# Decoder layer on one core: other portions in TensorE's written order, and the output weights split once and kept in DRAM

## The chip, the cores and the metric

The kernel runs on one core of one Trainium2 chip. The metric is the device time of one execution in microseconds (us). Before the change the median of three runs is 2806.22 us (2804.65 to 2808.27).

## What is computed

One layer of a hybrid decoder on 2048 tokens of width 1024, in float32:

```python
h = rmsnorm(x)
hg_p, rw_p = split(h @ w_in)              # 1024 x 3840, 30 column tiles of 128
o_hg = hgrn2(hg_p)                        # 4 heads, chunkwise gated linear recurrence
o_rw = rwkv7(token_shift_mix(rw_p))       # 8 heads, chunkwise, inverse of a triangular 64x64 matrix
x = x + concat(o_hg, o_rw) @ w_out        # 1024 x 1024
x = x + conv_ffn(rmsnorm(x))              # up to 2 x 2816, conv of width 3, SiLU gate, down
return rmsnorm(x)
```

Every large product is made of three products: an operand is split into `hi` (a cast to float32r on ScalarE) and `lo` (the rest, a subtraction on VectorE), and `mm3` adds hi x hi, hi x lo and lo x hi. One such triple of 128x512 matmuls is called a dense step below.

## The kernel before

The first part of the kernel (`phase1`, some 1,420 of 2,806 us) interleaves three Python generators: `dense()` (the input projection, block by block of 512 tokens, and for the first three blocks the output projection `out_block`), `rw_stream()` (eight "supers", two in each token block, of the RWKV recurrence) and `hg_stream()` (sixteen units of the HGRN recurrence). The second part (output projection of the last block, feed-forward, final norm) isn't touched by the change.

**Order.** TensorE's instructions stand in the order in which the generators emit them; a scheduling layer places those of the other engines, whose queues then run in order too. The loop at the end of `phase1` takes one step of the RWKV stream and one of the HGRN stream, and then lets `fill` emit dense work for `FLOOR + RATE * (work of these steps)` ns, 900 + 0.45 times. The work is a count kept by the wrapper `Metered`: `V.ns` grows by 150 ns + 1.04 ns an element for each VectorE instruction and by half of that for each ScalarE `act`; and at the two places where `rw_super` sends data through DRAM `V.ns += TRIP_NS` adds 8,000.

**The inverse's round trips.** In `rw_super`, VectorE masks the scores into `M` (from TensorE's line 737). Pieces of `M` go to DRAM and come back as `E` (lines 753, 756: first trip). Thirty-one pairs of VectorE instructions (`etmp`, `Ti`) invert the triangles; `Ti` goes to DRAM and comes back as `TZ` and `TTs` (lines 815 to 828: second trip), and then TensorE goes on at line 836. Between the two trips stand the transposes `KBT` (line 763), those of `AT` (772) and the product `lv` (789), which don't need `E`.

**The output projection.** `out_block` runs over two halves of the block's tokens (`i2`), two halves of the columns (`dh`) and eight k tiles. For each k it loads a tile of w_out (128x512 float32, 256 KB, line 409, by GpSimd's DMA queue), splits it on ScalarE (line 269) and VectorE (line 80), and makes two dense steps with it. So each block loads and splits 32 tiles, the three blocks 96. The pool gives four buffers each to the raw tile, `wh` and `wl`. The rows of `oT` (the recurrences' output) are split as they come in.

**The input projection.** In the first token block `load` reads two raw tiles of 256 KB for each column tile, splits them and stores hi and lo as `Win` in DRAM (four stores of 256 KB); the later blocks load the split tiles. All of these go by GpSimd's queue. SyncE's queue carries the rest, in program order.

## Time and profile before

| | |
|---|---|
| median of 3 runs | 2806.22 us |
| the profiled execution | 2807.51 us |
| its span, first to last instruction | 2805.7 us |
| mean granted TensorE clock | 0.971 |
| TensorE / VectorE / ScalarE busy | 94% / 68% / 49% |
| DMA, mean over the span | 184 GB/s |

All places in time are microseconds from the span's start. "PE" is TensorE, "DVE" VectorE, "ACT" ScalarE, "POOL" GpSimd, "SP" SyncE; DMA queue q0 is GpSimd's and q1 SyncE's. A window row has the window, its length, the busy time of PE, weight loads, DVE, ACT and POOL with instructions in brackets, the granted clock as a share of full speed, the share of the 16 DMA engines in use, and GB/s. A matmul at half clock counts as busy for its longer time, so the time that a window loses on TensorE is its idle time plus length x (1 - clock).

### The profile page before, as it was taken

The page shows a single profiled execution, that of the slowest core. Times are in us where ns is not written, and L with a number is a line of the kernel's source. Part 1 is how long each engine was busy: PE and PEld are TensorE (multiplying, and loading weights), DVE is VectorE, ACT ScalarE, POOL GpSimd, SP SyncE. Part 2 cuts the span into 40 slices and gives each one's busy share as a digit, 9 for nine tenths or more (in the row PEclk, how much of TensorE's full clock was granted, in tenths as well). Part 3 has the DMA queues.
Part 4 walks back from the last instruction along what each step waited for, and adds up shares of the span by engine and source line. Part 5 has one row for each costly group of instructions (what it writes and reads, how often), then busy time and mean ns, then how long its engine had stood idle before and what let it go on. Part 6 is the DMA issues. An engine that isn't in the chain of part 4 may idle for free.

```text
span 2805.7 us, 47910 instructions
## 1 busy us (share of the span) xinstructions
PE 2643.6 (94%) x18059; PEld 2109.4 (75%) x18059; DVE 1910.3 (68%) x3665; ACT 1366.7 (49%) x2178; POOL 367.1 (13%) x660
## 2 busy tenths in 40 slices
PE   7989999998999989989789999998999999999998
PEld 5867777776777767767567888886888888877887
DVE  4856656476545664746667789988998777667656
ACT  4545543454544444434446765446555555445444
POOL 6432222112221122222100000000000000000000
PEclk9989999998999999989899999999999999999999
DMA  8654635346473455844556357755663223999865
GB/s 292 210 154 141 193 117 152 96 134 192 155 197 114 119 158 192 302 117 128 141 186 216 122 161 257 250 187 190 216 226 116 75 89 109 326 323 329 290 193 187
DMA packets 387709, 515.78 MB, mean 184 GB/s; under 512 B 121759, under 2 KB 218389, under 8 KB 387477
## 3 DMA queue, kind: packets, MB, share of 16 engines
q1 hardware_dynamic: 335537, 343.29, 38.5%
q0 software_dynamic: 51872, 169.41, 18.7%
q8 instruction: 142, 2.33, 0.3%
q14 instruction: 90, 0.74, 0.1%
q10 hardware_dynamic: 68, 0.02, 0.0%
HBM read 375.22 MB, written 137.36 MB: 183 GB/s over the span
## 4 chain that ended last, share of the span: by engine, by line
PE 41%; DMA 3%; DVE 3%; issue 1%; ACT 1%; SPq 1%; DVEq 0%; ACTq 0%
PE ua L285 5%; PE ua L287 5%; PE ua L286 5%; PE ud L285 3%; PE ud L286 3%; PE ud L287 3%; PE da L286 2%; PE da L287 2%; PE da L285 2%; PE db L285 2%; PE db L286 2%; PE db L287 2%; PE ub L285 1%; PE ub L287 1%; PE ub L286 1%
## 5 line engine op out<-in xcount | busy, mean ns | idle before, releaser
L285 PE MATMUL pj<-hh,wh 128*128 128x512 f32 x960 | 411.0, 428 | 0.1
L287 PE MATMUL pj<-hh,wl 128*128 128x512 f32 x960 | 380.2, 396 | 0.0
L286 PE MATMUL pj<-hl,wh 128*128 128x512 f32 x960 | 380.1, 396 | 0.0
L285 PE MATMUL ua<-Bh,uwh 128*128 128x512 f32 x704 | 278.5, 396 | 16.2 <-ACT uwh L269 14.1
L287 PE MATMUL ua<-Bh,uwl 128*128 128x512 f32 x704 | 276.5, 393 | 0.5 <-DVE uwl L80 0.4
L286 PE MATMUL ua<-Bl,uwh 128*128 128x512 f32 x704 | 276.1, 392 | 0.0
L285 PEld LDWEIGHTS pj<-hh,wh 128*128 128x128 f32 x960 | 183.6, 191 | 51.5 <-issue 8.8
L286 PEld LDWEIGHTS pj<-hl,wh 128*128 128x128 f32 x960 | 183.9, 192 | 41.0 <-issue 7.7
L287 PEld LDWEIGHTS pj<-hh,wl 128*128 128x128 f32 x960 | 183.2, 191 | 40.9
L269 ACT CAST uwh<-uraw 128x512 fp32r<-128x512 f32 x220 | 134.6, 618 | 145.4 <-PE ua L286 71.7
L269 ACT CAST dah<-draw 128x512 fp32r<-128x512 f32 x151 | 93.9, 622 | 184.5 <-PE da L286 50.5
L80 DVE TENSOR_TENSOR uwl<-uraw,uwh 128x512 fp32r<-128x512 f32 x220 | 146.7, 684 | 50.2 <-ACT uwh L269 50.1
L80 DVE TENSOR_TENSOR dal<-draw,dah 128x512 fp32r<-128x512 f32 x151 | 104.0, 689 | 103.9 <-ACT dah L269 103.5
L285 PEld LDWEIGHTS ua<-Bh,uwh 128*128 128x128 f32 x704 | 133.2, 189 | 45.7 <-ACT uwh L269 14.7
L287 PEld LDWEIGHTS ua<-Bh,uwl 128*128 128x128 f32 x704 | 133.2, 189 | 30.8 <-DVE uwl L80 2.8
L286 PEld LDWEIGHTS ua<-Bl,uwh 128*128 128x128 f32 x704 | 133.4, 190 | 26.9
L285 PE MATMUL ud<-Bh,uwh 128*128 128x512 f32 x352 | 137.9, 392 | 1.4 <-DVE cv L80 1.4
L287 PE MATMUL ud<-Bh,uwl 128*128 128x512 f32 x352 | 137.1, 389 | 0.0
L286 PE MATMUL ud<-Bl,uwh 128*128 128x512 f32 x352 | 137.0, 389 | 0.0
L80 DVE SCALAR_TENSOR_TENSOR y<-cv,cvt,y 128x1024 f32<-128x1024 f32 x88 | 112.5, 1278 | 33.9 <-ACT y L143 33.9
L286 PE MATMUL da<-dbl,dah 128*128 128x512 f32 x340 | 133.4, 392 | 1.1 <-DVE dbl L80 0.9
L287 PE MATMUL da<-dbh,dal 128*128 128x512 f32 x340 | 132.4, 390 | 0.0
(536 smaller groups left out, 6058.4 us busy)
## 6 DMA issues: line engine op xcount, KB each, us to landing
uraw<-in_w_up_dram SPq DMA_DIRECT2D x176, 256.0 KB, 3.2
woraw<-in_w_out_dram POOLq DMA_DIRECT2D x96, 256.0 KB, 3.4
draw<-Sg SPq DMA_DIRECT2D x88, 256.0 KB, 3.3
draw<-Tw SPq DMA_DIRECT2D x88, 256.0 KB, 5.3
gd<-y SPq DMA_DIRECT2D x86, 256.0 KB, 2.9
xt<-x1d SPq DMA_DIRECT2D x32, 512.0 KB, 5.9
draw<-gd SPq DMA_DIRECT2D x63, 256.0 KB, 4.5
draw<-in_w_down_dram SPq DMA_DIRECT2D x63, 256.0 KB, 5.4
```

The costliest lines, as they stand in the source:

```text
L80: return call(out_, *args, **kw)
L269: S.copy(hi, src)
L285: TE.matmul(acc, lh, rh, start=first, stop=False, skip_group_check=skip)
L286: TE.matmul(acc, lh, rl, start=False, stop=False, skip_group_check=skip)
L287: TE.matmul(acc, ll, rh, start=False, stop=last, skip_group_check=skip)
```

## The change

Three edits, all in `phase1`:

1. The portions. VectorE's count and ScalarE's are kept apart, ScalarE's in full, and the larger of the two counts. The trip's constant is 14,000 in place of 8,000, is added only at the second trip, and comes on top of the larger count.
2. `split_wout`, a new generator that is driven by one step for each dense step from the third column tile on: for each half `dh` it loads the 2 MB of w_out into the buffer tag of `M`, splits them into tiles of the tags `KBT`, `KB`, `UV` and `AR` (which the first super uses later) and stores them to `Wod` in DRAM, 1 MB a store, all by SyncE's queue. Each of the sixteen 128x512 pieces is split once.
3. `out_block` loads hi and lo of `Wod` (2 x 256 KB for each k, GpSimd's queue) and splits nothing of w_out. It takes k in pairs: both k for the first 128 tokens, then both for the second.

```diff
-OP_NS, ELEM_NS, TRIP_NS = 150.0, 1.04, 8000.0
+OP_NS, ELEM_NS, TRIP_NS = 150.0, 1.04, 14000.0
...
+    def take(self):
+        t_ = max(self.ns, self.act_ns) + self.wait_ns
+        self.ns = self.act_ns = self.wait_ns = 0.0
+        return t_
...
-        V.ns += 0.5 * (OP_NS + ELEM_NS * width(out_))
+        V.act_ns += OP_NS + ELEM_NS * width(out_)
...
-                        raw = wp.tile([P, 512], F32, tag="wraw", name="woraw", bufs=4)
-                        wload(raw, w_out[0, k * P:(k + 1) * P, dh * 512:dh * 512 + 512])
-                        wh, wl = split(wp, raw, [P, 512], "w", 4)
...
+                    for k2 in range(0, KD, 2):
+                        ws = []
+                        for k in (k2, k2 + 1):
...
+                            w = tuple(wp.tile([P, 512], F32R, tag="w" + c, name="wo" + c, bufs=4) for c in "hl")
+                            for t_, d_ in zip(w, Wod[dh][k // 4]):
+                                wload(t_.bitcast(F32), d_[:, k % 4, :])
+                            ws.append(w)
                         for q in range(2):
...
+                            for k, w in zip((k2, k2 + 1), ws):
...
+                                mm3(accs[q], lhs, w, k == 0, k == KD - 1)
...
+        def split_wout():
+            for dh in range(2):
+                raw = rp.tile([P, 8, BLK], F32, tag="M", name="wod")
+                for q in range(2):
+                    dma(raw[:, 4 * q:4 * q + 4, :],
+                        w_out[0, q * 512:q * 512 + 512, dh * 512:dh * 512 + 512].rearrange("(k p) c -> p k c", p=P))
+                for _ in range(8):
+                    yield
+                for q in range(2):
+                    hi, lo = (rp.tile([P, 4, BLK], F32R, tag=tag, name="wo" + c)
+                              for tag, c in ((("KBT", "h"), ("KB", "l")), (("UV", "h"), ("AR", "l")))[q])
+                    for k in range(4):
+                        split_to(hi[:, k, :], lo[:, k, :], raw[:, 4 * q + k, :])
+                        yield
+                    for t_, d_ in zip((hi, lo), Wod[dh][q]):
+                        dma(d_, t_.bitcast(F32))
...
+                    if i > 1:
+                        next(early, None)
...
-            V.ns += TRIP_NS          # after E<-Ed
...
-            V.ns += TRIP_NS          # after TTs<-T1d
+            V.wait_ns += TRIP_NS
...
-            fill(FLOOR + RATE * (V.ns - t0))
+            fill(FLOOR + RATE * V.take())
```

What this does to the queues is shown at three places.

ScalarE's queue in the first 40 us, before: `hh` are the eight evictions of the transposed first block, of which each dense step of the first column tile needs one, and `wh` the casts of input weights.

```order
L143 ACTIVATE hh<-hg,vt 128x512 x2
L143 ACTIVATE hh<-rw,vt 128x512 x4
L269 CAST wh<-wraw 128x512
L143 ACTIVATE hh<-hg,vt 128x512 x2
L269 CAST wh<-wraw 128x512
```

And after the change, where `woh` are the casts of w_out:

```order
L148 ACTIVATE hh<-hg,vt 128x512 x2
L148 ACTIVATE hh<-rw,vt 128x512
L267 CAST woh<-wod 128x512 x4
L148 ACTIVATE hh<-rw,vt 128x512
L267 CAST woh<-wod 128x512
L148 ACTIVATE hh<-rw,vt 128x512
L267 CAST woh<-wod 128x512 x3
L148 ACTIVATE hh<-rw,vt 128x512
L274 CAST wh<-wraw 128x512
L148 ACTIVATE hh<-hg,vt 128x512 x2
```

Eight casts of w_out now stand among the evictions that the first column tile waits for.

SyncE's queue at the start, before: after the constants come three small weights, the next token block's rows (`xt`) and then the first super's first trip (`Ed`).

```order
L514 DMA cst<-in_consts_dram 128x1344
L512 DMA w2a_195<-in_rw_w_dram 64x512
L513 DMA w2a_195<-in_rw_a_dram 64x512
L515 DMA g_196<-in_rw_g_dram 128x512
L437 DMA xt<-in_x_dram 128x1024 x4
L753 DMA Ed<-M 32x16x32 x4
```

And after it (`wod` are the loads of w_out, 1 MB each; `Wod` the stores, 128x2048 float32, 1 MB each):

```order
L544 DMA cst<-in_consts_dram 128x1344
L448 DMA wod<-in_w_out_dram 128x4x512 x2
L542 DMA w2a_195<-in_rw_w_dram 64x512
L543 DMA w2a_195<-in_rw_a_dram 64x512
L545 DMA g_196<-in_rw_g_dram 128x512
L459 DMA Wod00h<-woh 128x2048
L459 DMA Wod00l<-wol 128x2048
L459 DMA Wod01h<-woh 128x2048
L459 DMA Wod01l<-wol 128x2048
L448 DMA wod<-in_w_out_dram 128x4x512 x2
L467 DMA xt<-in_x_dram 128x1024 x2
L459 DMA Wod10h<-woh 128x2048
```

Three more stores and the other two `xt` follow: four loads and eight stores of 1 MB have come in ahead of the first super.

VectorE's queue where the first super begins, before: `W`, the first super's table of decays, is set at the very start of the program, since its buffer (tag `UV`) is free.

```order
L80 MEMSET eps_73 128x1
L80 MEMSET epsgn 128x1
L80 MEMSET rows 128x128
L80 MEMSET W 128x16
L80 MEMSET Sf 128x256
```

And after it, some 60 rows later, in the fifth and sixth column tile of the first block:

```order
L80 COPY lastc<-pj 128x1
L80 TENSOR_TENSOR wol<-wod,woh 128x512
L80 TENSOR_TENSOR wl<-wraw,wh 128x512 x2
L80 SCALAR_TENSOR_TENSOR rkv_621<-pj,vt,rkv_621 128x511
L80 SCALAR_TENSOR_TENSOR rkv_621<-lastc,vt,rkv_621 128x1
L80 COPY lastc<-pj 128x1
L80 TENSOR_TENSOR wl<-wraw,wh 128x512
L80 MEMSET W 128x16
L80 TENSOR_TENSOR wl<-wraw,wh 128x512
```

The `MEMSET W` has moved behind the last split of w_out (`wol`), and it needs the buffer from which `Wod11h` is stored, so that store has to be over before VectorE goes on to the next `wl`.

On TensorE the portions have moved as follows; the numbers are dense steps, counted in the written order, for supers 0 to 7:

| dense steps | before | after |
|---|---|---|
| between the transposes of KB and those of AT (the portion behind the first trip) | 8, 9, 0, 9, 8, 9, 8, 9 | 3, 3, 4, 4, 3, 3, 3, 3 |
| between `lv` and the product that needs `TZ` (line 836) | 43, 41, 40, 40, 43, 40, 43, 39 | 46, 43, 43, 43, 47, 42, 47, 41 |
| in all between the last scores (line 737) and line 836 | 65, 68, 58, 65, 64, 65, 65, 66 | 64, 64, 65, 64, 65, 62, 65, 62 |

Between the first and the last `etmp` of supers 3, 5 and 7 VectorE's queue held 16, 13 and 13 subtractions of w_out before and holds none after.

60 lines of the change are left out of this document (30 added, 30 removed).

## The prediction

> **What bounds the kernel now.** I read the page's first lines, then windows of the first part, then TensorE's waits in them, and then the DMA queues of the same windows. TensorE is the engine that everything else feeds:
>
> ```profile
> PE 2643.6 (94%) x18059; PEld 2109.4 (75%) x18059; DVE 1910.3 (68%) x3665; ACT 1366.7 (49%) x2178; POOL 367.1 (13%) x660
> ```
>
> So a change pays where it takes away TensorE's idle time, or time at half clock. The second part isn't touched. For the first, one quiet window, and the three windows in which the output projection of blocks 0, 1 and 2 runs:
>
> ```profile
> 1250.00:1320.00 70.00, 69.83 (x520) 52.49 (x517) 43.23 (x83) 29.70 (x40) 18.12 (x34) 1.00 0.40 128
> 581.00:673.00 92.00, 74.53 (x505) 56.12 (x505) 66.60 (x169) 42.05 (x65) 18.95 (x36) 0.91 0.60 169
> 965.00:1057.00 92.00, 75.60 (x876) 57.92 (x875) 64.08 (x163) 39.01 (x69) 17.91 (x34) 0.90 0.57 162
> 1329.00:1417.00 88.00, 73.56 (x872) 56.11 (x871) 56.72 (x149) 41.10 (x72) 14.14 (x27) 0.90 0.51 143
> ```
>
> The quiet window loses nothing. The three others are idle for 17.5, 16.4 and 14.4 us, and by their clock (0.91, 0.90, 0.90) lose another 8.3, 9.2 and 8.8: **74.6 us in all**; at full clock and without idle time they hold 66.2, 66.4 and 64.8 us of work. TensorE's waits over the whole first part name the sources:
>
> ```profile
> PE rw L836 <- DMA TZ<-T0d: 40.7, 12, 10.1
> PE pj L285 <- ACT wh L269: 16.2, 8, 5.3
> PE pj L286 <- DVE wl L80: 7.0, 15, 2.4
> PE rw L886 <- ACT UV L143: 5.7, 2, 3.1
> ```
>
> The first row is the inverse's second trip (12 waits, 40.7 us, the longest 10.1), the next two are the split of weights. The same waits in the first and second block's windows alone:
>
> ```profile
> PE rw L836 <- DMA TZ<-T0d: 0.7, 1, 0.7
> ...
> PE rw L836 <- DMA TZ<-T0d: 3.9, 1, 3.9
> ```
>
> So only some 5 of the trip's 40.7 us lie in the blocks: the blocks and the trips are two stores of lost time. An idle spell also costs clock: the window after super 0's trip runs at 0.61, that of super 6 at 0.60.
>
> ```profile
> 148.00:165.00 17.00, 6.56 (x87) 5.71 (x86) 2.49 (x8) 3.37 (x7) 3.11 (x5) 0.61 0.74 181
> 1200.00:1217.00 17.00, 7.32 (x84) 5.81 (x82) 3.35 (x12) 3.04 (x7) 1.82 (x4) 0.60 0.64 137
> ```
>
> **Part 1: no split of w_out in the blocks.** Removed are 96 casts and 96 subtractions, less 16 of each that are made once:
>
> ```profile
> L409 POOL DMA_DIRECT2D woraw<-in_w_out_dram x96: 537/537/539, 306.9 to 1416.8; - x96
> L269 ACT CAST wh<-woraw x96: 597/619/627, 572.3 to 1420.1; 128x512 fp32r<-128x512 f32 x96
> L80 DVE TENSOR_TENSOR wl<-woraw,wh x96: 628/691/694, 574.0 to 1420.8; 128x512 fp32r<-128x512 f32 x96
> ```
>
> That is 80 x 0.619 = 50 us of ScalarE and 80 x 0.691 = 55 us of VectorE. Neither bounds by itself, but both queues run in order and VectorE is nearly full just where the inverse needs it:
>
> ```profile
> 618.40:660.90 42.50, 38.00 (x115) 0.92 0.52 161
> 792.40:818.40 26.00, 24.50 (x91) 1.00 0.56 191
> ```
>
> The first row is VectorE from the first to the last `etmp` of super 3, beside output block 0: 38.00 of 42.50 us busy. The second is super 4, without a block: 24.50 of 26.00. The sixteen subtractions that leave the first stretch are 16 x 0.69 = 11 us; in supers 5 and 7 thirteen leave, 9 us. So TensorE's waits for weights and the inverse's chain get shorter together, by similar amounts.
>
> What takes the place is DMA. Each k brings 512 KB where 256 KB came. The DMA rows of the three windows (packets, MB, share of the 16 engines):
>
> ```profile
> q0 software_dynamic: 2767, 9.05, 31.9%
> q1 hardware_dynamic: 12257, 6.39, 27.5%
> ...
> q0 software_dynamic: 2640, 8.65, 30.8%
> q1 hardware_dynamic: 12256, 6.16, 25.2%
> ...
> q0 software_dynamic: 2154, 7.06, 26.8%
> q1 hardware_dynamic: 12420, 5.42, 23.6%
> ```
>
> A block's 32 further tiles are 8.39 MB on q0. For the time that this needs there are two rates. By the windows' own (block 0: 0.319 x 92 = 29.3 us for 9.05 MB) q0 would need 56.5, 55.8 and 51.6 us. By the full stretch from 33 to 63 us, where 349 GB/s went at a share of 0.97, so 360 GB/s at 1.00 (row in part 2), it needs 48.4, 47.3 and 42.9. With q1's own 25.3, 23.2 and 20.8 us the DMA engines want 82, 79 and 72 us at the first rate and 74, 71 and 64 at the second, against TensorE's 66, 66 and 65. So **the blocks turn from waiting for the split to waiting for DMA**, and can't shrink to TensorE's own work. I take the middle of the two rates, 78 + 75 + 68 = 221 us, and 9 us more for the trips: with TensorE 13 to 20 us earlier in each block but the chain only 9 to 11 us shorter, some 2 us of wait at line 836 come back, three times, and half as much again in clock. 272 - 230 = **42 us won**. The bounds: 272 - 197 - 9 = 66 us if the transfers hide wholly; 272 - 233 - 9 = 30 at the slower rate. The pairs of k hold a buffer for three of four dense steps, so the loads can't start earlier than that; this is in the same bounds.
>
> **Part 2: the early copy.** The change adds 4 loads and 8 stores of 1 MB, 12.6 million bytes, on SyncE's queue before the first super. What the DMA engines do there:
>
> ```profile
> 21.00:33.00 12.00, 11.03 (x48) 7.72 (x47) 6.33 (x9) 5.46 (x10) 5.32 (x9) 1.00 0.56 178
> 33.00:63.00 30.00, 30.00 (x134) 24.83 (x133) 13.27 (x29) 12.17 (x21) 20.15 (x33) 1.00 0.97 349
> 63.00:69.00 6.00, 6.00 (x27) 3.81 (x26) 3.36 (x6) 3.79 (x7) 2.97 (x6) 1.00 0.81 274
> 69.00:81.00 12.00, 12.00 (x48) 8.54 (x47) 11.33 (x15) 11.89 (x15) 3.46 (x7) 1.00 0.37 127
> ```
>
> From 33 to 63 us TensorE is never idle, and the DMA engines are full with the loads and `Win` stores that keep it fed. Free before 63 us are 0.44 x 12 + 0.03 x 30 = 6.2 us, at 360 GB/s 2.2 MB. `MEMSET W` stands in VectorE's queue ahead of the next input weights and waits for the store of `Wod11h`, so all but that last store's successor (1 MB) must be over there; two of four `xt` loads (1 MB) move behind. 12.6 - 2.1 - 2.2 = 8.3 MB have no room: 23 us at 360 GB/s, which TensorE waits, since its own weights share the engines. The eight casts among the `hh` evictions (8 x 0.62 = 5 us) lie within the same wait. I take **20 us lost**, as the copies can use moments in which the other queue waits. The bounds: 35 us if nothing overlaps (12.6 / 0.360), 8 us if the room from 63 to 81 us (1.1 + 7.6 us) and one buffered column tile (8 dense steps of 0.67 us, 30.00 / 134 x 3) cover the rest.
>
> **Part 3: the portions.** The dense work is the same in sum; it moves between places. What covers both trips together goes from 516 to 511 steps over the eight supers, so the "longer portion" at the second trip is paid for by the one taken away at the first. Outside the blocks' supers (0, 1, 2, 4, 6) the cover changes by -1, -4, +7, +1 and 0 steps, +3 x 0.67 = 2 us, half as much again for clock: **3 us won**, between -10 (every step lost at a wait, none gained) and +12 (the seven steps of super 2 all meet its wait, 4.7 us, and take its clock along, and 4 and 6 gain about as much by a lighter VectorE).
>
> **Sum.** 2807.5 (the profiled execution, span 2805.7) - 42 + 20 - 3 = 2782.5. This execution lies 1.3 us above the median shown, so 2781; I say **2782 us**.
>
> **Two rules that speak against it.** GpSimd issues twice as many loads. The Trainium skill, "SBUF — State Buffer", section "SBUF: two separate sides", says that VectorE in some modes keeps GpSimd from writing the descriptors of its DMAs. By that rule the 64 issues of a block would be stretched beside a full VectorE. The rows say otherwise here: 96 issues took 537 to 539 ns each, in stretches with VectorE 89% busy. I give it no term. The skill's "DMA: Bandwidth & Descriptors", section "Where 436 GB/s comes from", puts the limit of transfers from HBM at about 358 GB/s and that of the fabric at 435; by the first the blocks stay bound by DMA as worked out above, by the second they would hide and the first rival below would hold. The trace's 349 GB/s agrees with the first, as a mean over 30 us.
>
> **The rivals.**
>
> ```profile
> GB/s 229 382 421 426 404 344 290 404 388 415 410 382 426 355 371 415 361 404 333 300 404 300 322 388 350 300 366 344 328 361 333 268 344 344 257 322 350 262 180 382
> ```
>
> *The transfers hide.* For it: in the window from 33 to 63 us several slices of 0.75 us carried over 400 GB/s, as the row shows, and the loads run ahead by two k. Against: at both rates the shares above come to more than TensorE's work nearly everywhere. It gives 2807.5 - 66 + 8 - 3 = 2747. Chance 0.15.
>
> *The inverse takes the place of the weights.* The blocks shrink only by what VectorE is relieved, 11 + 9 + 9 = 29 us, and TensorE waits the rest at line 836. For it: the chain of super 3 is as long as TensorE's path. 2807.5 - 29 + 20 - 3 = 2795.5. Chance 0.15.
>
> *The early copy costs all of its bytes, and the blocks run at the slower rate.* 2807.5 - 30 + 35 - 3 = 2809.5, no change. Chance 0.12.
>
> *The weights land too late: slower.* A pair of k gives its buffers back at three quarters of its four steps, and they are wanted again two pairs later; with a block's 66 us over eight such rounds a load may take 8.3 x 5/8 = 5.2 us, less one issue 4.7. Landing times before:
>
> ```profile
> DMA to landing us min/median/max: 2.8/3.4/6.7
> ...
> Win171l<-wl POOLq DMA_DIRECT2D x1, 256.0 KB, 8.1
> ```
>
> The first row is `woraw`'s, with room; the second a `Win` store of 256 KB in the full stretch. Each us above 4.7 costs 24 rounds x 1.5 (clock) = 36 us. From 6.1 us on (the 66 + 3 - 20 = 49 us that would else be won, by 36, above 4.7) the change loses; at 6.5 us the time is 2807.5 - 66 + 65 + 20 - 3 = 2823, at 7 us 2841. Chance 0.18.
>
> The forecast itself keeps 0.40. Differences under 0.2%, 5.6 us, can't be told from no change. Faster: the forecast (nearly all of it), the first two rivals and a little of the third: 0.68. Same: most of the third and edges of the others: 0.13. Slower: 0.19. The range of 2750 to 2822 us takes in the bounds of the blocks and of the early copy and the near end of the last rival.
>
> **What would show it.** Right: windows of the output blocks of 74 to 80 us with a DMA share above 0.8 and no waits for casts; `etmp` stretches near 30 us in supers 3, 5 and 7; TensorE idle some 20 us before 100 us with a DMA share near 1, and VectorE idle ahead of `W`. Wrong: TensorE not idle early (the copies hid), or block windows as long as now with waits on `woh` and `wol` for DMA (the last rival) or on `TZ` (the second).

## The result, and the profile after

| | before | after |
|---|---|---|
| median of 5 runs | 2806.22 us (2804.65 to 2812.06) | 2822.57 us (2814.95 to 2825.03) |
| ratio, 95% interval | 1 | 1.0048 [1.0030, 1.0067] |
| the profiled execution | 2807.51 us | 2814.95 us |
| its span / mean granted clock | 2805.7 us / 0.971 | 2813.1 us / 0.975 |

The kernel became slower by 0.3 to 0.7%, where 24 us were forecast to be won. The profiled execution of after is the fastest of its five, so its span is only 7.4 us longer than that of before; a second profile of the same kernel (`changed_again` below) has 2821.0 us, and its stretches differ by no more than 5 us from those read here.

The page's first line has the engines' busy time in the whole execution:

```profile
PE 2639.5 (94%) x18059; PEld 2101.1 (75%) x18059; DVE 1861.9 (66%) x3585; ACT 1320.3 (47%) x2096; POOL 418.6 (15%) x756
```

The work that was to go is gone: VectorE has 48.4 us less, ScalarE 46.4. TensorE has the same. So the question is what TensorE waits for now. I cut the first part at the first matmul of each super (`rw<-tl,w2a`), which the change doesn't touch, and compare stretches. Windows of before from the starts of supers 3, 5 and 7 to those of 4, 6 and of the second part, in which the three output blocks lie, and the same of after:

```profile
550.90:741.70 190.80, 173.18 (x1530) 131.74 (x1529) 114.94 (x264) 87.01 (x134) 38.96 (x73) 0.94 0.54 160
897.20:1112.50 215.30, 195.29 (x1649) 151.10 (x1648) 120.92 (x283) 94.32 (x149) 45.04 (x84) 0.94 0.52 158
1277.20:1445.00 167.80, 147.52 (x1447) 111.60 (x1446) 106.17 (x249) 75.14 (x119) 27.86 (x52) 0.95 0.47 141
```

```profile
565.20:754.50 189.30, 167.70 (x1515) 127.23 (x1513) 94.69 (x232) 70.79 (x102) 56.05 (x106) 0.95 0.66 203
903.80:1117.90 214.10, 193.93 (x1658) 148.95 (x1656) 102.35 (x253) 73.83 (x115) 63.20 (x119) 0.96 0.63 198
1278.70:1449.40 170.70, 149.47 (x1458) 112.63 (x1456) 87.78 (x220) 53.60 (x84) 47.62 (x89) 0.96 0.62 189
```

The second column is the length: 573.9 us before, 574.1 after. **The blocks' stretches won nothing.** Length less TensorE's busy time is 57.9 us before and 63.0 after; length times the missing clock is 32.7 and 24.9. The whole span adds up like this (after minus before): +16.9 us up to the start of super 1; -2.6 in supers 1 and 2, -6.2 in super 4 and -3.9 in super 6, which hold no block; +0.2 in the three blocks' stretches; +4.9 between the first two weights of the second part (`wacc` to `ua`); -1.8 after that.

TensorE's waits of the whole first part, after; shown are the second trip, the cast of `hh` and all rows with block weights (total us, times, longest):

```profile
PE rw L868 <- DMA TZ<-T0d: 26.5, 7, 8.1
PE pj L290 <- DMA woh<-Wod11h: 12.5, 7, 6.4
...
PE pj L290 <- ACT hh L267: 7.8, 1, 7.8
...
PE pj L290 <- DMA woh<-Wod10h: 4.9, 5, 2.2
PE pj L291 <- DMA wol<-Wod10l: 4.0, 5, 1.7
...
PE pj L291 <- DMA wol<-Wod11l: 3.2, 7, 1.2
PE pj L291 <- DMA wol<-Wod01l: 3.0, 3, 1.4
...
PE pj L290 <- DMA woh<-Wod01h: 2.4, 4, 1.3
...
PE pj L290 <- DMA woh<-Wod00h: 0.9, 1, 0.9
```

The casts' rows (16.2 and 7.0 us before) are gone, and in their place stand 30.9 us of waits for `woh` and `wol` to land. The waits for the inverse's second trip fell from 40.7 to 26.5 us, but not in the blocks: in their three stretches they were 4.6 us and are 3.6. The landing times of these loads, and of `woraw` before, are in the groups of their lines:

```profile
DMA to landing us min/median/max: 3.1/4.9/7.9
```

Before they were 2.8/3.4/6.7. The DMA engines are not full meanwhile; windows inside the three blocks (the column before the last is the DMA share), and GpSimd's queue in the first of them:

```profile
590.00:690.00 100.00, 82.23 (x651) 62.48 (x650) 53.74 (x151) 27.53 (x42) 36.08 (x69) 0.91 0.84 247
965.00:1070.00 105.00, 88.58 (x972) 66.69 (x971) 53.10 (x155) 26.49 (x47) 36.14 (x68) 0.95 0.75 230
1329.00:1420.00 91.00, 75.26 (x921) 56.75 (x919) 41.77 (x128) 21.74 (x42) 32.42 (x61) 0.96 0.75 228
```

```profile
q0 software_dynamic: 5388, 17.65, 57.5%
```

17.65 MB took 57.5 us of full share, 307 GB/s: the slower of the two rates that the prediction used. But the longest wait has another reason than the rate. GpSimd's queue at the end of block 0, and TensorE's matmul behind it:

```profile
670.59 0.54 POOL L616 DMA_DIRECT2D wl<-Win280l  x1 [5.10 <-PE pj L291]
671.12 0.54 POOL L616 DMA_DIRECT2D wh<-Win280h  x1
672.04 0.54 POOL L616 DMA_DIRECT2D wh<-Win281h  x1 [0.38 <-PE pj L292]
672.57 0.54 POOL L616 DMA_DIRECT2D wl<-Win281l  x1
674.11 0.54 POOL L417 DMA_DIRECT2D woh<-Wod11h  x1 [1.01 <-PE pj L292]
674.64 0.54 POOL L417 DMA_DIRECT2D wol<-Wod11l  x1
```

```profile
680.93 0.79 PE L290 MATMUL pj<-woh,hh 128*128 128x512 f32 x1 [6.44 <-DMA woh<-Wod11h]
```

The call `last()` fetches the next column tile's weights (`Win280`, `Win281`) at k = 5 of the last pass, as it did before. In the trace of before one load of the block, 256 KB, stands behind these four on GpSimd's queue. Now k = 5 is the second of a pair whose successors, k = 6 and 7, haven't been asked for, and each k has two loads. So the column's four loads stand ahead of the block's own last four, and take two of the four buffers. TensorE sat idle for 6.44 us.

In block 2 the longest wait is another queue's. ScalarE and SyncE's queue there:

```profile
1376.53 1.57 ACT L148 ACTIVATE TZ<-rw 32x256 f32<-32x256 f32 x4 [10.58 <-DMA TTs<-T1d]
1383.85 1.10 ACT L267 CAST hh<-oraw 128x256 fp32r<-128x256 f32 x3 [5.75 <-DMA oraw<-oT]
```

```profile
1375.16 1.73 SPq L437 DMA_DIRECT2D x1d<-xh  x2
1376.94 8.60 SPq L413 DMA_DIRECT2D oraw<-oT  x6
```

The loads of `oraw` stand behind the block's own stores of `x1d`, which wait for TensorE; the cast of `hh` starts at 1383.85, and TensorE waits 7.8 us for it. The start of the second part has a longer wait (1.66 us before), and ScalarE has the same 5.4 us ahead of it, for the last store of `yo`:

```profile
PE wacc L291 <- DVE wol L80: 5.4, 1, 5.4
```

```profile
ACT woh L267 <- DMA oT<-yo: 5.4, 1, 5.4
```

The early copy, last, in three of the windows that the prediction read:

```profile
33.00:63.00 30.00, 24.99 (x101) 19.60 (x99) 13.51 (x28) 11.84 (x21) 12.51 (x21) 0.94 1.03 397
63.00:69.00 6.00, 5.26 (x16) 4.30 (x17) 3.67 (x9) 3.20 (x6) 4.53 (x8) 0.72 1.02 421
69.00:81.00 12.00, 10.67 (x47) 7.63 (x47) 2.16 (x6) 1.21 (x2) 4.48 (x7) 1.00 1.02 400
```

From 33 to 81 us the DMA engines are full and TensorE, which was never idle there, is idle for 7.1 us. VectorE waits for the store of `Wod11h` ahead of `W`:

```profile
74.29 0.07 DVE L80 MEMSET W<- 128x16 f32 x1 [4.83 <-DMA Wod11h<-woh]
```

Super 0 starts 10.9 us later than before (76.4 us in place of 65.5); the other 6 of the 16.9 us come within it (171.8 us in place of 165.6).

### The profile page after: what moved, and what is told of

It reads as the page before. It is cut to its first block, busy times and chain, and to the rows that moved or that the text cites. A ratio compares the mean times of both kernels' runs of the same rounds, so it can differ in the third digit from the quotient of the medians.

```text
span 2813.1 us, 47681 instructions
## 1 busy us (share of the span) xinstructions
PE 2639.5 (94%) x18059; PEld 2101.1 (75%) x18059; DVE 1861.9 (66%) x3585; ACT 1320.3 (47%) x2096; POOL 418.6 (15%) x756
## 3 DMA queue, kind: packets, MB, share of 16 engines
q0 software_dynamic: 59552, 194.58, 21.2%
## 4 chain that ended last, share of the span: by engine, by line
PE 63%; DMA 12%; DVE 10%; issue 8%; ACT 3%; POOL 3%; SPq 1%; DVEq 0%; POOLq 0%; ACTq 0%
PE pj L290 6%; PE pj L291 5%; PE pj L292 5%; PE ua L290 5%; PE ua L292 5%; PE ua L291 5%; PE ud L290 2%; PE ud L291 2%; PE ud L292 2%; PE da L291 2%; PE da L292 2%; PE da L290 2%; PE hg L1036 1%; DMA wraw<-in_w_in_dram 1%; PE db L291 1%
## 5 line engine op out<-in xcount | busy, mean ns | idle before, releaser
L291 PEld LDWEIGHTS pj<-hl,wh 128*128 128x128 f32 x960 | 183.4, 191 | 40.5 <-issue 7.7
L274 ACT CAST dah<-draw 128x512 fp32r<-128x512 f32 x151 | 93.8, 621 | 182.7 <-PE da L291 52.3
```

Source lines behind the costliest of these rows:

```text
L274: S.copy(hi, src)
L291: TE.matmul(acc, lh, rl, start=False, stop=False, skip_group_check=skip)
```

## The experiments

All kernels were timed in alternation with the kernel before, at different times, in which its median was 2805.2 to 2810.8 us. So two kernels are compared by their ratios to before. The changed kernel was timed twice, with ratios of 1.0048 and 1.0056, in the middle 1.0052; "less than after" below is the difference to this, times 2806 us, and the intervals make it good to some 5 us.

The columns behind the ratio come from one profiled execution, cut as above: its time, the start of super 1, the supers without a block (1, 2, 4, 6), the three blocks' stretches, and `wacc` to `ua`. The two profiles of the changed kernel differ by up to 2.4 us in these. An execution can lie further from its kernel's median: that of next_weights_behind is 13 us below it, that of mended_old_portions 10.

| kernel | median us | ratio to before, 95% | profiled us | super 1 starts | supers 1, 2, 4, 6 | blocks | wacc to ua |
|---|---|---|---|---|---|---|---|
| before | 2806.2 | 1 | 2807.5 | 231.1 | 640.0 | 573.9 | 52.5 |
| after | 2822.6 | 1.0048 [1.0030, 1.0067] | 2815.0 | 248.0 | 627.3 | 574.1 | 57.4 |
| changed_again | 2821.9 | 1.0056 [1.0036, 1.0075] | 2822.8 | 249.1 | 629.7 | 576.1 | 57.6 |
| portions_alone | 2803.3 | 0.9979 [0.9968, 0.9991] | 2804.0 | 228.5 | 639.0 | 574.0 | 52.2 |
| copy_and_loads | 2837.9 | 1.0115 [1.0096, 1.0133] | 2842.5 | 249.0 | 641.3 | 587.6 | 57.2 |
| trip_only | 2820.4 | 1.0040 [1.0027, 1.0054] | 2817.8 | 239.9 | 637.1 | 575.0 | 57.6 |
| no_early_copy | 2784.7 | 0.9921 [0.9902, 0.9940] | 2779.3 | 230.3 | 628.0 | 560.5 | 52.9 |
| buffers_in_place | 2809.9 | 1.0020 [1.0006, 1.0034] | 2807.7 | 247.9 | 628.0 | 573.1 | 52.3 |
| one_weight_pair | 2761.6 | 0.9845 [0.9830, 0.9860] | 2761.6 | 245.9 | 630.2 | 517.3 | 58.2 |
| loads_unread | 2826.7 | 1.0085 [1.0063, 1.0107] | 2828.3 | 245.6 | 633.3 | 580.5 | 56.7 |
| next_weights_behind | 2810.3 | 1.0007 [0.9993, 1.0021] | 2797.3 | 248.0 | 628.6 | 558.1 | 56.6 |
| one_k_at_a_time | 2807.6 | 1.0011 [0.9999, 1.0022] | 2808.1 | 249.3 | 630.2 | 564.0 | 56.7 |
| one_k_next_behind | 2807.5 | 1.0004 [0.9992, 1.0016] | 2803.2 | 249.9 | 629.7 | 558.2 | 56.0 |
| five_weight_buffers | 2817.8 | 1.0042 [1.0029, 1.0054] | 2817.8 | 252.2 | 632.3 | 568.8 | 56.2 |
| rows_together | 2806.6 | 1.0006 [0.9996, 1.0015] | 2811.5 | 249.5 | 633.2 | 564.2 | 55.7 |
| all_mended | 2795.3 | 0.9963 [0.9950, 0.9975] | 2791.6 | 247.6 | 629.4 | 551.4 | 53.3 |
| mended_old_portions | 2805.8 | 0.9985 [0.9974, 0.9996] | 2795.6 | 246.2 | 639.0 | 551.3 | 52.0 |
| copy_spread_out | 2801.6 | 0.9984 [0.9969, 0.9999] | 2793.3 | 227.4 | 646.0 | 559.8 | 51.7 |
| copy_in_block_0 | 2813.3 | 1.0026 [1.0015, 1.0037] | 2810.8 | 230.0 | 630.6 | 591.4 | 51.8 |
| copy_in_row_buffer | 2787.9 | 0.9939 [0.9922, 0.9956] | 2791.7 | 230.3 | 644.5 | 554.5 | 52.8 |

### Which of the three parts

**portions_alone**: the kernel before with the first edit alone (lines of `Metered`, `act`, the two trips and `fill`).

> The kernel before with the portions of the change and nothing else of it (w_out is split in the blocks as before). Theory A (the portions are the part that wins: between the end of super 0 and the start of block 0, and in supers 4 and 6, TensorE caught up 3.8 + 8.6 + 4.6 = 17 us in the changed kernel's trace): 12 to 20 us faster than before, 2786 to 2794. Rival (the prediction's term: the cover only moves; what was caught up came from a lighter VectorE): 0 to 6 us faster, 2800 to 2806.

It took 2803.3 us, a ratio of 0.9979: some 6 us won, 3 to 9 by the interval. That is the rival, the prediction's term. The portions didn't make the change slow.

**copy_and_loads**: the changed kernel without that edit.

```diff
-OP_NS, ELEM_NS, TRIP_NS = 150.0, 1.04, 14000.0
+OP_NS, ELEM_NS, TRIP_NS = 150.0, 1.04, 8000.0
-        V.act_ns += OP_NS + ELEM_NS * width(out_)
+        V.ns += 0.5 * (OP_NS + ELEM_NS * width(out_))
```

(and `TRIP_NS` added at both trips).

> The changed kernel with the old portions: the early copy and the blocks' loads of split weights stay. Theory A (copy costs 17, blocks win nothing, portions had won 17): 12 to 22 us slower than the changed kernel, 2828 to 2840. Rival (the portions do little): within 6 us of the changed kernel's 2815 to 2825.

2837.9 us. Copy and loads alone cost 32 us; the blocks' stretches are 13.7 us longer than before, and those without a block 1.3 us longer. So the new portions are worth some 18 us beside the loads and 6 beside the split. TensorE's waits for the second trip, over the whole first part, are as long as before, though the blocks split nothing:

```profile
PE rw L869 <- DMA TZ<-T0d: 42.1, 9, 10.0
```

**no_early_copy**: `split_wout` isn't run, and the blocks load tiles of `Win` in place of `Wod`, so three output blocks are computed with other weights.

```diff
-                            for t_, d_ in zip(w, Wod[dh][k // 4]):
-                                wload(t_.bitcast(F32), d_[:, k % 4, :])
+                            for t_, d_ in zip(w, stage["Win"][8 * dh + k][0]):
+                                wload(t_.bitcast(F32), d_.rearrange("p k c -> p (k c)"))
-            early = split_wout()
+            early = iter(())
```

> The changed kernel without the early copy; the blocks load as many tiles of the same size, but of the split input weights (Win), so the output projection of the first three token blocks is computed with other weights. The prediction's term: 15 to 22 us faster than the changed kernel, 2800 to 2808, and the first super's first matmul back at 66 us from 76. Rival (TensorE would wait in the same places for other reasons): under 8 us faster.

2784.7 us, 37 less than after, more than either theory had. Super 1 starts at 230.3 us, 17.7 earlier, and `wacc` to `ua` is 52.9: both are the early copy's. The blocks' stretches are 13.6 us shorter as well, which the copy can't explain by itself, since it is over long before. That led to two of the questions below, on the layout of `Wod` and on the copy's buffers.

### What the blocks wait for

**one_weight_pair**:

```diff
-                        ws = []
+                        if k2 == 0:
+                            ws = []
                         for k in (k2, k2 + 1):
...
+                            if k2 == 0:
+                                w = tuple(wp.tile([P, 512], F32R, tag="w" + c, name="wo" + c, bufs=4) for c in "hl")
...
+                                ws.append(w)
```

> The changed kernel, but each pass of an output block (two row tiles by half of the columns) loads its weights only for k = 0 and 1 and uses these two tiles for all eight k. It leaves out three quarters of w_out, so the output is another one; the number of matmuls, the early copy and the portions stay. The blocks lose 32, 29 and 25 us in the changed kernel (idle time and half clock). Theory A: what is left of these losses is the arrival of the weights (bandwidth, the order of GpSimd's queue, the buffers). Then three quarters of the loads less take away some 30 to 45 us: 2780 to 2792 us. Rival B: TensorE would wait there for the inverse and for the other block's stores and loads in any case, and the weights only come first in the records: under 10 us are won, 2813 us or more.

2761.6 us, 58 less than after, more than theory A had. It leaves out three quarters of w_out. The three stretches, to be held against those of after above:

```profile
562.70:730.00 167.30, 159.42 (x1515) 124.94 (x1513) 93.57 (x232) 70.41 (x102) 30.53 (x58) 0.98 0.50 154
881.60:1074.70 193.10, 183.94 (x1658) 144.60 (x1656) 102.28 (x253) 73.73 (x115) 37.74 (x71) 1.00 0.51 154
1236.50:1393.40 156.90, 143.15 (x1458) 111.33 (x1456) 87.50 (x220) 53.66 (x84) 21.88 (x40) 0.97 0.42 125
```

The same matmuls (1515, 1658 and 1458), with VectorE and ScalarE as busy as in after, take 56.8 us less: TensorE's idle time is 30.8 us in place of 63.0, and the clock is 0.97 to 1.00. Rival B (the inverse and the stores take over) falls. What the split took from TensorE could have been won, and the loads of the split weights take it.

**loads_unread**: the same loads, and nobody waits for them.

```diff
-                                mm3(accs[q], lhs, w, k == 0, k == KD - 1)
+                                mm3(accs[q], lhs, (hh[:, k, :], hl[:, k, :]), k == 0, k == KD - 1)
```

> The changed kernel, but in the output blocks TensorE takes hh and hl as its weights: the loads of the halves go on as before, into the same buffers and on the same queue, and nothing reads them. It leaves out w_out, so the output is another one. With nobody to wait for, the loads run ahead in a burst. Theory A (only the arrival ahead of the matmul costs): blocks 0 and 1 run as in the kernel with one pair of weights a pass, 2762 to 2775 us. Rival B (the bytes are the price, by slowing the other transfers: oT, x, the inverse's trips): 2790 us or more. Block 2 may lose some us, since its own hh is written while it is read here.

2826.7 us: theory A falls in this form. Two windows of block 0, and TensorE's longest waits in blocks 0 and 1:

```profile
594.00:633.00 39.00, 36.38 (x308) 29.74 (x304) 13.03 (x30) 14.96 (x21) 24.66 (x46) 1.00 1.02 373
640.00:674.00 34.00, 20.60 (x162) 16.75 (x164) 27.43 (x95) 2.44 (x4) 5.56 (x10) 0.73 0.46 163
```

```profile
PE pj L290 <- DVE xh L80: 22.1, 1, 22.1
```

```profile
PE rw L868 <- DMA TZ<-T0d: 25.7, 2, 23.0
```

The loads ran in a burst at 373 GB/s with a share of 1.02. TensorE was 93% busy at full clock during it; the price is what it waited behind the bursts: 22 us for `xh` and, in block 1, 23 us for `TZ`. Both go back to the inverse's round trips. The addition that makes `xh` stood in VectorE's queue behind an `etmp`, and that waited for the first trip:

```profile
640.41 0.19 DVE L80 TENSOR_TENSOR etmp<-E,Ti 128x31 f32<-128x31 f32 x1 [24.66 <-DMA E<-Ed]
```

So bytes that nobody waits for cost too, by the transfers of other chains. This doesn't tell what the same bytes cost when TensorE paces them.

**next_weights_behind**: the call behind the loads of the last pair.

```diff
                                 mm3(accs[q], lhs, w, k == 0, k == KD - 1)
+                                if i2 == 1 and dh == 1 and q == 0 and k == KD - 2 and last is not None:
+                                    last()
                                 if i2 == 1 and dh == 1 and q == 1:
                                     next_block(then, k)
-                                    if k == KD - 3 and last is not None:
-                                        last()
```

> The changed kernel with one call moved: the loads of the next column tile's input weights are issued behind the block's last four weight tiles in place of ahead of them. Theory B (the order on GpSimd's queue: in block 0 TensorE waits 6.4 us for Wod11h, which stands behind four loads of Win): 8 to 14 us faster than the changed kernel, waits for woh in block 0 under 3 us. Rival C (the DMA engines are simply full, share 0.84 in block 0, so the wait moves to the next column tile): within 4 us of the changed kernel.

2810.3 us, 13 less than after. The waits for `woh` and `wol` fall from 30.9 to 21.9 us. The profile's blocks are 16.0 us shorter, but this execution is the fastest of its twelve. The order of GpSimd's queue is a cause.

**one_k_at_a_time**: the loop over k as before, loads and `last()` as in after.

```diff
-                    for k2 in range(0, KD, 2):
-                        ws = []
-                        for k in (k2, k2 + 1):
+                    for k in range(KD):
...
                         for q in range(2):
...
-                            for k, w in zip((k2, k2 + 1), ws):
```

> The changed kernel with the order of the k in a block as it was before (k by k, both row tiles for each) instead of pairs of k; the loads stay as changed, 512 KB of split weights for each k, and so does the call for the next column's weights. A tile of weights is then free again six dense steps before it is wanted, not five. Theory A (the landing time against the round of the buffers decides, as the prediction's fourth rival priced it: one step, 1.0 us of a round, is 36 us while landing takes longer than the round, less near its end): 10 to 30 us won, 2793 to 2812 us. Rival B (one stall a block decides, the next column's loads that stand ahead of the last pair's in GpSimd's queue; k by k it is nearly the same stall): within 6 us of the changed kernel, 2817 to 2828 us.

2807.6 us, 12 less than after, and 10.1 in the blocks. The waits for `woh` and `wol` fall from 30.9 to 14.3 us, though the loads land no sooner (5.0 us in the median): a tile that is free one step earlier is asked for one step earlier. So how early a buffer comes free is a cause too.

**one_k_next_behind**: both edits.

> Both: k by k, and the next column's weights called for behind the loads of the last k. The call alone took the changed kernel from 2822.6 to 2810.3 us. If the two add up (theory A for the order of k): 2785 to 2800 us. If the call was all (rival B): 2806 to 2813 us.

2807.5 us, 13 less than after: the rival by its time, no more than either edit alone. The waits for weights are down to 9.8 us, the blocks to 558.2. The two don't add up: they shorten the same waits, and part of what they free stands elsewhere (5.2 us for `xh` in block 0, 6.7 us for `hh` in block 2). With one k at a time the place of the call is worth 2 us, which can't be told from nothing.

**five_weight_buffers**: `bufs=5` for `wh`, `wl`, `woh`, `wol`, and 3 in place of 4 for the raw tiles.

> The changed kernel with five buffers for each half of the weights instead of four, paid for by three instead of four of the raw tiles (oraw, xh, h2, the first columns' raw weights). Bytes, order and queues stay. Taking three quarters of the blocks' loads away won 61 us, so the loads are the cause; open is whether it is their number of bytes or the time that each has to land. Theory A (time to land against the round of the buffers): a fifth buffer adds one k to the round, some 2 us, more than the 0.3 us by which the median landing passes the round, so 15 to 35 us are won: 2788 to 2808 us. Rival B (the bytes: TensorE waits for DMA bandwidth however many loads are under way): under 6 us, 2817 to 2826 us, with waits on woh and wol as before. Three raw tiles can cost some us in the first columns, which the start times of the supers would show.

2817.8 us, 3 less than after, which can't be told from nothing. The waits for weights fall to 13.2 us, as theory A has it, but the three raw tiles take most of it back: super 1 starts 4.2 us later, and waits for `hh`, `hl` and `xh` grow from 9.8 to 18.8 us. By time alone this would have looked like rival B; the waits show that a fifth buffer does let the weights come in time.

**rows_together**: the rows of one k in one piece of DRAM.

```diff
-dp.tile([P, 4, BLK], F32, name=f"Wod{dh}{q}{c}")
+dp.tile([4 * P, BLK], F32, name=f"Wod{dh}{q}{c}")
-                                wload(t_.bitcast(F32), d_[:, k % 4, :])
+                                wload(t_.bitcast(F32), d_[k % 4 * P:k % 4 * P + P, :])
```

> The changed kernel with another layout of Wod in DRAM: the 128 rows of one k lie together (256 KB in one piece) instead of four k side by side in each row (pieces of 2 KB, 8 KB apart). In the kernel that took its block weights from tiles of Win, which lie together, the loads landed after 3.1 to 4.1 us in block 0 against 4.5 to 5.7. If the layout is the reason: the landing times fall below 4.5 us and 8 to 20 us are won, 2802 to 2815 us. If not (there the copy's buffers or other things made the difference): within 5 us of the changed kernel.

2806.6 us, 13 less than after; the median landing over the blocks is 4.4 us in place of 4.9, the waits for weights 21.2 us, the blocks 564.2. The bytes, the packets on this queue (4,096 bytes in both traces) and the queue are the same, so where the rows lie in DRAM matters. Why is open.

### What the early copy costs

**buffers_in_place**: the copy takes its tags in the order `KBT`, `M`, `UV`, (`WC`), `AR`, (`BV`), `KB`, in which the first super took them in the kernel before.

> The changed kernel with the early copy's buffers taken in the order in which the kernel before first takes these tags, so that every buffer of the supers lies where it lay before. Theory: the 5 us that the changed kernel loses at the start of the second part (57.4 instead of 52.5 us between its first two weights, a wait of 5.4 us for the store of yo) come only from the moved places: that stretch goes back to 52 to 53 us, and the time to some 2817 us. Rival: the early copy itself or the blocks' order do it: 57 us stay. The supers' own waits may change by 1 or 2 us either way with the places.

`wacc` to `ua` goes back to 52.3 us: the 5 us were those of moved places. The copy had made the pool give out addresses in another order, and the second part's first buffers came to lie where `yo` lies until it is stored (the row of ScalarE above). By the ratios it is 9 us less than after, of which this explains 5; the other 4 are within what can be told, and the profile's other stretches are the same within 2 us.

**copy_spread_out**: the copy in 128x256 pieces during the second token block's columns, in one pair of buffers, and the call behind.

> The changed kernel with the next column's weights called for behind the last pair's loads, and with the copy of w_out moved from the time before the first super into the columns of the second token block, when the DMA engines are little used: half a tile (128x256) at a time in two buffers of its own, loads and stores on SyncE. Everything is computed. Without any copy the changed kernel took 2784.7 us, and the call is worth 12. Theory: the 17 us of the early copy were the price of its place and the 5 us at the start of the second part that of its buffers, not of its bytes; then 2768 to 2785 us. Rival: the bytes cost wherever they go (12.6 million, 35 us at 360 GB/s at most), or its stores on SyncE hold up the inverse's trips: 2795 us or more.

2801.6 us, far from the 2768 to 2785 expected: super 1 starts at 227.4 us, and supers 1, 2, 4 and 6 take 646.0 us, 17.4 more than with the call alone. ScalarE's waits from 225 to 420 us:

```profile
ACT coh L267 <- DVE col L80: 17.4, 8, 5.2
...
ACT coh L267 <- DMA Wod00h<-coh: 7.8, 4, 2.9
ACT coh L267 <- DMA Wod10h<-coh: 7.5, 2, 4.1
```

The next cast waits for the one pair of buffers, and the evictions behind it on ScalarE wait too.

**copy_in_block_0**: block 0 splits as before and stores both halves by GpSimd's queue; blocks 1 and 2 load them; k by k, the call behind.

```diff
+                        if nb == 0:
+                            raw = wp.tile([P, 512], F32, tag="wraw", name="woraw", bufs=4)
+                            wload(raw, w_out[0, k * P:(k + 1) * P, dh * 512:dh * 512 + 512])
+                            w = split(wp, raw, [P, 512], "w", 4)
+                            if i2 == 0:
+                                for t_, d_ in zip(w, Wod[dh][k // 4]):
+                                    wload(d_[:, k % 4, :], t_.bitcast(F32))
```

> No early copy: output block 0 loads and splits w_out as the kernel before does, k by k, and stores both halves in its first half (32 stores of 256 KB on GpSimd's queue); blocks 1 and 2 load the stored halves, k by k, with the next column's weights called for behind the last k. New portions. Everything is computed. Worked out from runs: 2806.5 before, less 4 for the portions, less 11 for the stretch from super 5 to the end of block 2 as in the kernel without an early copy, less some 3 for k by k there; block 0 as before and some 5 for its stores: 2790 to 2798 us. Rival: the stores (8.4 MB) make block 0's raw loads land too late or hold its buffers, and TensorE waits 15 us and more there: 2803 us or more.

2813.3 us: the rival. Block 0's stretch takes 213.7 us in place of 189.3, and its waits are the split's again, longer than before:

```profile
PE pj L290 <- ACT wh L274: 18.8, 12, 2.9
PE pj L291 <- DVE wl L80: 6.3, 13, 2.0
```

The stores stand on GpSimd's queue between the raw loads and wait there for the split; GpSimd's largest wait in block 0:

```profile
POOL Wod01h L420 <- ACT wh L274: 20.4, 4, 6.6
```

So the next raw load is issued late, and the next split comes late with it.

### Sums and controls

**changed_again**: the changed kernel once more.

> The changed kernel itself once more, beside the three kernels that follow, since five kernels with one edit each came out 5 to 16 us below its first median. If that median (2822.6 us) stands, 2818 to 2825 us; if it was drawn high, 2812 to 2818 us, and each edit is worth that much less.

2821.9 us: the first median stands.

**all_mended**: k by k, the call behind, the rows of one k together, the copy's buffers in place; the early copy stays.

> The changed kernel with its early copy, and four edits together: k by k, the next column's weights called for behind the last k, the rows of one k of Wod together, the copy's buffers in the order of before. Alone they gave 15 (the first two together), 16 and 13 us. Theory A (the first three act on one thing, TensorE's wait for the arrival of weights, of which 31 us are left in the changed kernel and 10 with the first two; the fourth is worth 5 us at the start of the second part): 2793 to 2801 us. Rival B (what is left is the DMA engines' bytes): 2802 to 2808 us.

2795.3 us, a ratio of 0.9963 [0.9950, 0.9975] to before: theory A. The waits for weights are 7.3 us, the blocks 551.4. Four edits that gave 9 to 13 us each give 25 together. It is still 34 us above the kernel with one pair of weights a pass, though its largest waits in the blocks are now for `hh` (9.2 us) and `xh` (8.5), and no longer for weights.

**copy_in_row_buffer**: these edits, but the copy in the second token block's columns, in the 16 KB that the next rows use later.

```diff
+            t_ = xp_.tile([P, 2, 4, 512], F32R, tag="xt", name="wos", bufs=1)
+            for n in range(16):
+                dh, k, s_ = n // 8, n % 8, n % 4
...
+                split_to(t_[:, 0, s_], t_[:, 1, s_], raw)
```

> As all_mended, but without the early copy: the copy of w_out runs in the columns of the second token block, in the buffer of the next rows, which is free there (16 KB, four slots of both halves), so that ScalarE's casts need not wait for a store as they did in copy_spread_out (39 us in 17 waits). Everything is computed. Theory (the early copy's 17 us are the price of its place, copy_spread_out's 14 us in supers 1 and 2 that of ScalarE's waits): 2778 to 2790 us. Rival (12.6 MB more in supers 1 and 2 hold up the inverse's trips and the Win loads whatever the buffers): 2793 us or more.

2787.9 us, a ratio of 0.9939 [0.9922, 0.9956]: the fastest of the kernels here that compute everything. The copy still costs: supers 1, 2, 4 and 6 take 644.5 us in place of 629.4. TensorE's longest wait of super 1 is the inverse's trip:

```profile
PE rw L861 <- DMA TZ<-T0d: 11.6, 1, 11.6
```

So the 17 us at the start were largely the price of the copy's bytes and casts, 15 of which come back beside super 1; what its moving saves is some 3 us there. The gain over all_mended (ratios 0.9939 and 0.9963, 7 us) is near what can be told; the two profiled executions are equal.

**mended_old_portions**: all_mended with the portions of before.

> all_mended with the portions of before (8 us at both trips, ScalarE's work half in VectorE's sum). The new portions were worth 4 us in the kernel before and 15 in the changed one. Theory A (they cover waits that only the relieved engines of the changed kernel leave: VectorE and ScalarE have less in their portions once the casts are gone): 10 to 16 us are lost again, 2805 to 2811 us, part of them in supers without a block. Rival B (they covered waits for late weights, which the mends have taken away): under 5 us, 2795 to 2800 us.

Ratio 0.9985 in place of 0.9963, some 6 us lost: between the two theories. The blocks' stretches are the same (551.3 and 551.4), the supers without a block 9.6 us longer, and the waits for the second trip 40.5 us in place of 24.8. The profiled execution lies 10 us below its median, so the sizes are rough. Beside mended weights the portions pay by the inverse's waits, not by the weights'.

**trip_only**: the new trip constant, ScalarE's count as before.

```diff
-        V.act_ns += OP_NS + ELEM_NS * width(out_)
+        V.ns += 0.5 * (OP_NS + ELEM_NS * width(out_))
```

> The changed kernel with one half of the portions' edit: 14 us at the second trip and nothing at the first, but ScalarE's work added half to VectorE's sum, as before. If the trips alone carry the 15 us: 2817 to 2825 us. If ScalarE's full count does: 2830 us or more. Between these each has a part.

2820.4 us, a ratio of 1.0040: the same as after, so by its time the trips carry the 18 us. The stretches show more: super 1 starts 8.1 us earlier than in after, and the supers without a block take 9.8 us longer, with the waits for the second trip nearly back at those of before:

```profile
PE rw L868 <- DMA TZ<-T0d: 38.1, 9, 10.5
```

So in these two profiles the full count of ScalarE's work costs 8 us and wins 10.

## Why the prediction was wrong, step by step

**What bounds the kernel: right.** TensorE's idle time and half clock in the blocks and at the trips were the two stores of lost time. With the loads mostly taken away the blocks' stretches gave 56.8 us, and the 66 us of its upper bound weren't far.

**Part 1, what is removed: right.** 46 us of ScalarE and 48 of VectorE went, 50 and 55 were forecast. The inverse's chain got shorter where a block runs beside it: from the first to the last `etmp` supers 3, 5 and 7 take 33.3, 29.6 and 25.0 us in place of 41.7, 41.1 and 41.6; some 30 were forecast. The fall of the trip's waits from 40.7 to 26.5 us isn't this part's alone: copy_and_loads, without the split too, has 42.1.

**Part 1, what takes the place: here it failed.** The step is "the blocks turn from waiting for the split to waiting for DMA ... I take the middle of the two rates, 78 + 75 + 68 = 221 us, and 9 us more for the trips: 42 us won". It priced the DMA engines' total work, as if they could be kept full; the stretches won 0 of the 42, and with the old portions they lost 13.7 (copy_and_loads). The 9 us for the trips were nothing either: their waits in the blocks' stretches were 4.6 us and are 3.6. The measured share was 0.84, 0.75 and 0.75. TensorE was held by single loads, and the runs show three reasons that the sum of bytes doesn't have: GpSimd's queue has the next column's loads ahead of the last pair's (13 us); in pairs a tile is asked for a step later than k by k (12 us, largely the same waits); and the stored rows lie 8 KB apart (13 us). All mended, with the copy's buffers put back, the blocks' stretches win 22.5 us against before, and 34 more go when three quarters of the loads do. The rewritten loop also asks for `xh` two k earlier, and adds and stores each row tile by itself; no run takes this alone.

The sentence on the pairs' later loads, "this is in the same bounds", was the slip: a bound by rate says nothing about when each load may start. And the order of GpSimd's queue was not looked at past the block's own loads, though the change doubled what stands on it.

**The rivals.** "The weights land too late" named the mechanism and was given 0.18; its sign, waits on `woh` and `wol` for DMA, is what came. Its price was wrong: it let a load take 4.7 us before anything is lost, and the change lose from 6.1 us on. The median was 4.9 us, by which 7 us would have been lost; the waits were 30.9. A median hides the loads of 6 to 8 us, and k by k the waits halved at a median of 5.0. "The inverse takes the place of the weights" is refuted by one_weight_pair, and by the 3.6 us of the trip's waits in the blocks. "The transfers hide" is refuted by the waits for the loads, and by loads_unread: even with nobody waiting the bytes cost.

**Part 2: right in size, in part by luck.** 20 us were forecast and 16.9 measured by the start of super 1, with TensorE idle, VectorE waiting ahead of `W` and the DMA share at 1.02. But only 10.9 us stand ahead of super 0, and TensorE's idle time from 33 to 81 us is 7.1, where some 20 before 100 us were to be seen. The other 6 fall in super 0, which the prediction doesn't treat; trip_only, with the same copy, lacks them (165.9 us), so they depend on the portions too. (The lower bound of 8 us is 8.9 by its own terms.) It also left out that the copy moves the pool's places (5 us at the start of the second part).

**Part 3: right alone, too small in company.** 3 us were forecast and some 6 measured alone; in the changed kernel it was 18, above the bound of 12, in the mended one some 6. The supers without a block gain only where the portions and the relief of Part 1 stand together: they take 640.0 us before, 639.0 in portions_alone, 641.3 in copy_and_loads, 637.1 in trip_only and 627.3 in the changed kernel. So a term that depends on Part 1 was added as if it didn't. Why the two need each other stays open.

**The sum.** 2807.5 - 0 in the blocks' stretches, + 17 for the early copy, - 13 in the supers without a block, where 3 were forecast, + 5 for the moved places and - 2 in the rest gives 2814.5, the profiled execution (2814.95). The range ended at 2822 us, 0.6 below the median.

## What to carry to other kernels

Where split operands are stored and loaded again, the bytes double, and the question isn't only whether the DMA engines have room for them: for each load, write down when its buffer comes free, what stands ahead of it on its queue, and when it is wanted. A new buffer user ahead of the others can move every later buffer of a pool. And a prefetch call that stands at a fixed k has to be looked at again when the loads behind it change: that one line was worth 13 us with k in pairs, and nothing that could be told with one k at a time.

## What the runs showed of the hardware

**The rate.** Before the change 349 GB/s over 30 us was the highest long row, and the prediction weighed a limit of 358 by it. With more to move, loads and stores together, the same 30 us carried 397 GB/s, the next 6 us 421, and the burst of loads_unread 373 over 39 us. The Trainium skill, "HBM Reference", section "Specifications (TRN2)", says that a core that streams alone gets well above its share of 358 GB/s, and gives some 425; these rows agree with that, and not with 358 as a limit for one core. In the blocks the rate at full share was 307 GB/s all the same.

**The clock.** A wait of TensorE in after, and single microseconds behind it (the clock is the third column from the end):

```profile
63.74 0.77 PE L290 MATMUL pj<-hh,wh 128*128 128x512 f32 x1 [2.87 <-DVE lastc L80]
```

```profile
64.00:65.00 1.00, 1.00 (x3) 0.81 (x3) 0.79 (x2) 0.71 (x2) 0.89 (x2) 0.50 1.00 406
65.00:66.00 1.00, 1.00 (x3) 0.72 (x3) 0.45 (x1) 1.00 (x3) 0.91 (x2) 0.50 1.03 430
66.00:67.00 1.00, 1.00 (x4) 0.79 (x3) 1.00 (x3) 0.10 (x1) 1.00 (x3) 0.50 0.96 406
```

After an idle spell of 2.87 us the granted clock was 0.50 for 3 us, which costs half as much again. Not every such spell does it: in before TensorE waited 2.59 us up to 1027.07 us, and the clock stayed at 1.00. The Trainium skill, "TensorE: Matmul & The Clock Gate", section "What's actually happening", lets the clock drop after an idle window of some 3.4 us; by this row a shorter spell is enough.

**The layout in DRAM.** With packets of 4,096 bytes in both, loads of 256 KB whose rows lie together landed in 4.4 us in the median, those with rows 8 KB apart in 4.9, and the kernel was 13 us faster. Beside the other mends it was the same: 4.3 us in all_mended, 5.0 in one_k_next_behind.
